# A list planner's cost table: durations from the traces, form changes, a shared port, and a smaller reserve for matmuls

## The chip, the cores and the metric

The kernel runs on one core of a Trainium2 chip. The metric is the device time of one execution in microseconds; of the kernel before, three runs gave a median of 1301.49 us (1301.43 to 1301.89). The engines are named as in the profile: PE (TensorE, matmuls), PEld (its weight loads), DVE (VectorE), ACT (ScalarE), POOL (GpSimd) and SP (SyncE, which issues the DMAs). Each engine works off its own instructions strictly in the order in which the program was written for it, and waits where an input isn't there yet.

## The reference

A residual block of a language model, on 512 tokens of width 1024. Two token mixers run side by side on the normalised input: HGRN2 (8 heads of 128, a gated linear recurrence computed in chunks of 32) and RWKV-7 (16 heads of 64, a recurrence with a rank-one correction of the state). Their outputs are projected, gated by sigmoids, summed and projected again; a residual and a gated ConvFFN follow. Cut to what matters here:

```python
z = xn @ w_in                                   # all projections of both mixers and the gates
# HGRN2: q, f, v, g -> o_a, chunkwise with decays
y_a = (rmsnorm(o_a) * silu(hg)) @ w_branch_a
# RWKV-7, one step:
sa = einsum('bhvk,bhk->bhv', state, a_t)
state = state * w_t + sa[..., None] * b_t + v_t[..., None] * k_t
y = einsum('bhvk,bhk->bhv', state, r_t)
y_b = ((groupnorm(y) + bonus) * g) @ w_branch_b
h = x + rmsnorm((sigmoid(ga) * y_a + sigmoid(gb) * y_b) @ w_out)
out = h + rmsnorm((silu(gate) * val) @ w_down)  # gate, val = causal conv of rmsnorm(h) @ w_up
```

## The kernel before

Channels lie on the 128 partitions, the 512 tokens in the free dimension. Large products are made in three matmuls with operands split into a high and a low part in a reduced fp32 type (F32R): high x high, high x low, low x high. A weight block of 128 columns arrives by DMA (`raw`), ACT casts it to `whi_t`, POOL subtracts to get `wlo_t` in two halves of 512, and 24 matmuls of 512 columns (`zps`; for the HGRN values 256 columns, `vps`) accumulate one PSUM bank. Matmuls on plain fp32 operands appear as two records each.

The program has an opening part in fixed order, a **first planned stage** (`plan.run()`, L1206), the branch projections (`yps`) in fixed order, a **second planned stage** (`plan.run()`, L1371) with the output projection (`mix`), the norms and the first blocks of the FFN, and the FFN in fixed order.

In a planned stage, the work is written as generators that run beside each other and yield one operation at a time. Those of the first stage, in order of rank (L52): `chain` (L880), `evac` (PSUM out of the projections, L1135), `solve` (L818), `front` (L702), `hgrn` (L976), `split`, `load`, `gemm` (the projections, L1155). The 16 RWKV heads go in 8 pairs, called heads here:

- `front(hb)` makes the decays, norms and scaled keys on DVE and ACT, and scores `sc` by matmuls with 64 rows; its second half waits for `chain(hb - 2)`, whose buffers `X` it reuses.
- `solve(hb)` inverts the triangular part: 14 steps of small DVE operations (`tmp`, `nb`), then four groups of small matmuls (`fps`, `dps`, `fps2`, `dps2`).
- `chain(hb)` walks 8 chunks of 64 tokens. `vp` (transposes) opens it. Each chunk has two matmuls `zy` (of `sv`), a copy to `zs` by DVE and ACT, one matmul `us` (of `zs` and `qd`), its scaling into `sv` by DVE and ACT, two matmuls `sy` (of `sv`), and their sum into the next `sv` on DVE. ACT also makes the products `sp` and copies the results to `ys` and `yb`. All the matmuls of a chunk turn through the slots of two PSUM tiles, named `us` and `yp`, 8 slots each; a matmul's record carries the tile's name. They are 128 by 128 weights by 64 columns, with the unused half of `sv` at zero. After the chunks come the group norm, `yt`, `gps`.
- `gemm` yields the projections of all heads, and at the end those of the two output gates: the first (8 blocks) is released three chunks before the end of chain 6, the second by chain 7 in the same place.

`Plan` (L78) decides the order in which the engines get these operations. `prepare` (L129) finds when an operation's inputs are ready in planned time: the end of each writer, plus `HOP` for the pair of engines (L84), plus, for a matmul whose input comes from another engine, a reserve `MARGIN` (L46). `cost` (L152) gives a planned duration. `start` (L188) is the later of ready and the engine's planned free time. `run` (L211) takes, over all generators, the operation with the least start less a bonus (L53: chain on DVE 0.3, ACT 0.2, PE 0.05 us), ties by rank; `emit` (L191) advances the engine's planned time, records the end for later readers, and issues the instruction for real, behind the last one of its engine (`seq`, L316). The planned times go nowhere else: they fix only the order of instructions on each engine.

Of the kernel before, what the change touches and what calls it, by code (L numbers as in the profile page):

```python
# [11 lines left out]
ALU = mybir.AluOpType  # L12
# [4 lines left out]
P = 128  # L17
# [25 lines left out]
NWIN = 66  # L43
NX = 2
RAWS = 1
MARGIN = 0.6  # L46
AT0 = (3, 2, 4)
XG = ((0, 0),)
MORD = ((0, 0), (1, 0), (2, 0), (3, 0), (0, 1), (1, 1), (2, 1), (3, 1))
# [8 lines left out]
class Op:  # L58
    def __init__(self, key, fn, name, args, kw):
        self.key, self.fn, self.name, self.args, self.kw = key, fn, name, args, kw  # L60
        acc = [a for n, a in kw.items() if n == "accum_out"]
        pos = [a for a in args if isinstance(a, bass.AP)]
        self.outs = pos[:1] + acc
        self.ins = pos[1:] + [a for n, a in kw.items() if isinstance(a, bass.AP) and n != "accum_out"]
        self.bounds = []
        self.ready = None
# [11 lines left out]
class Plan:  # L78
# [8 lines left out]
    def __init__(self, seq, ranks, bonus, at, gaps=False):  # L87
        self.seq, self.ranks, self.bonus, self.gaps = seq, ranks, bonus, gaps
        self.at = dict(zip("TVAGD", at))
        self.dma = 0.0  # L90
        self.wide = True
        self.hist = {}
        self.procs = []
        self.n = 0
        self.now = 0.0
# [33 lines left out]
    def prepare(self, op):  # L129
        t = 0.0  # L130
        for aps, write in ((op.outs, True), (op.ins, False)):
            for ap in aps:
                key, b = self.bound(ap)
                op.bounds.append((key, b, write))
                for c, end, eng, w in self.hist.get(key, ()):
# [4 lines left out]
                    if hit:  # L140
# [3 lines left out]
                        if op.key == "T" and eng != "T":  # L144
                            lag += MARGIN
                        elif eng == "T" and len(op.ins) > 1 and op.ins[1].free_size() == 1:
# [5 lines left out]
    def cost(self, op):  # L152
        out = op.outs[0]
        n = out.free_size()
        scalars = sum(a.free_size() == 1 for a in op.ins) if n > 1 else 0
        far = any(a.space == PSUM for a in op.ins + op.outs)
        if op.key == "T":
            n, m = op.args[2].free_size() if op.name == "matmul" else n, op.args[1].free_size()
            if op.args[1].dtype == F32R:
                op.us = n / 2400 + 0.0022  # L160
            elif op.name == "transpose":
                op.us = 0.109 if n == 128 else 0.055
            elif n == 64 and m == 64:
                op.us = 0.111 if out.offset < 64 * out.ap[0][0] else 0.0535
            elif n == 64 and m == 128:
                op.us = 0.112
            elif n == 32:
                op.us = 0.044 if m == 32 else 0.155
            else:
                op.us = 0.218  # L170
            op.wide = n > 64 or m > 64
        elif op.key == "V":
            if op.name == "tensor_reduce":
                n = op.ins[0].free_size()
            rate = 160 if op.name == "reciprocal" else 960
            if op.name in ("tensor_copy", "tensor_scalar", "tensor_single_scalar") and not far:
                rate = 1920
            op.us = 0.069 + n / rate + 0.061 * scalars
        elif op.key == "A":
            op.us = (0.051 if far else 0.093) + n / 1200 + (0.093 if scalars or len(op.outs) > 1 else 0.0)  # L180
        elif op.key == "G":
            op.us = 0.147 + n / (470 if op.name == "tensor_tensor" else 840)
            if op.kw.get("op") == ALU.pow:
                op.us = 0.3 + n * 0.165
        else:
            op.us = 0.475

    def start(self, op):  # L188
        return max(op.ready, self.at[op.key])

    def emit(self, op, start):  # L191
        end = start + op.us
        if op.key == "T":
            wide = op.wide
            if wide and not self.wide and start < self.at["T"] + 0.05:
                end += 0.053
            self.wide = wide
        self.at[op.key] = end
        if op.key == "D":
            a = op.outs[0]  # L200
            self.dma = max(end + 0.625, self.dma) + math.prod(a.shape) * 4 / 360e3
            end = self.dma + 0.9
        for key, b, write in op.bounds:
            h = self.hist.setdefault(key, [])
            if write and b is not None:
                h[:] = [e for e in h if not (b[0] <= e[0][0] and e[0][1] <= b[1] and b[2] <= e[0][2]
                                             and e[0][3] <= b[3] and b[4] in (None, e[0][4]))]
            h.append((b, end, op.key, write))
        op.ins_ = self.seq(op.key, op.fn(*op.args, **op.kw))  # L209
# [37 lines left out]
def block_kernel(ctx: ExitStack, tc: tile.TileContext, out: bass.AP, xT: bass.AP, xN: bass.AP,  # L247
# [74 lines left out]
    def mm3(o, lh, ll, rh, rl, start, stop):  # L322
        T.matmul(o, lh, rh, start=start, stop=False)  # L323
        T.matmul(o, lh, rl, start=False, stop=False)  # L324
        T.matmul(o, ll, rh, start=False, stop=stop)  # L325
# [1202 lines left out]
```

## Time and profile before

| | us |
|---|---|
| median of three runs | 1301.49 |
| the profiled execution, its own time | 1302.32 |
| its span, first to last instruction | 1300.6 |
| PE busy in the span | 1235.4 |
| DVE busy | 717.4 |
| ACT busy | 575.5 |
| POOL busy | 532.5 |
| mean granted clock of the PE | 0.959 |

The span is 1.7 us shorter than the execution's own time, which has what lies before the first and after the last instruction. Busy time of the PE counts a matmul from its start to its modelled end; since matmuls are pipelined, the next starts well before that end, and the distance of two starts says more. A clock of 0.959 is the mean over stretches at full and at half speed.

### The profile page before, as it was taken

The page shows a single profiled execution, that of the slowest core. Times are in us where ns is not written, and L with a number is a line of the kernel's source. Part 1 is how long each engine was busy: PE and PEld are TensorE (multiplying, and loading weights), DVE is VectorE, ACT ScalarE, POOL GpSimd, SP SyncE. Part 2 cuts the span into 40 slices and gives each one's busy share as a digit, 9 for nine tenths or more (in the row PEclk, how much of TensorE's full clock was granted, in tenths as well). Part 3 has the DMA queues.
Part 4 walks back from the last instruction along what each step waited for, and adds up shares of the span by engine and source line. Part 5 has one row for each costly group of instructions (what it writes and reads, how often), then busy time and mean ns, then how long its engine had stood idle before and what let it go on. Part 6 is the DMA issues. An engine that isn't in the chain of part 4 may idle for free.

```text
span 1300.6 us, 19101 instructions
## 1 busy us (share of the span) xinstructions
PE 1235.4 (95%) x7140; PEld 999.3 (77%) x7140; DVE 717.4 (55%) x1491; ACT 575.5 (44%) x1257; POOL 532.5 (41%) x444
## 2 busy tenths in 40 slices
PE   8889899999999998999798999999999999999998
PEld 6677678777778776687686788888888888888886
DVE  7988876786876968767646321334543222323213
ACT  5533464654646546354454443223544343333321
POOL 5443333252232414123042446441366675655731
PEclk9889998999999989769699999999999999999999
DMA  5122112212112112111222364337333233322432
GB/s 178 42 66 84 41 54 68 57 49 64 56 58 71 58 41 72 32 49 35 54 70 66 108 201 123 93 94 239 133 98 98 74 121 90 105 82 81 116 111 81
DMA packets 54060, 110.97 MB, mean 85 GB/s; under 512 B 21584, under 2 KB 24784, under 8 KB 53968
## 3 DMA queue, kind: packets, MB, share of 16 engines
q1 hardware_dynamic: 53968, 109.75, 27.6%
q8 instruction: 57, 0.93, 0.3%
q14 instruction: 35, 0.29, 0.1%
HBM read 100.29 MB, written 9.44 MB: 84 GB/s over the span
## 4 chain that ended last, share of the span: by engine, by line
PE 72%; DVE 15%; ACT 6%; issue 4%; POOL 2%; DMA 1%; SPq 0%; DVEq 0%; POOLq 0%; ACTq 0%
PE zps L209 17%; PE zps L323 6%; PE zps L325 6%; PE zps L324 6%; PE us L209 4%; PE dn L325 3%; PE dn L323 3%; PE dn L324 3%; PE mix L209 3%; PE sc L209 3%; PE yp L209 2%; PE vps L209 2%; PE yps L323 2%; PE yps L325 2%; PE yps L324 2%
## 5 line engine op out<-in xcount | busy, mean ns | idle before, releaser
L209 POOL TENSOR_TENSOR wlo_t<-raw,whi_t 128x512 fp32r<-128x512 f32 x134 | 184.9, 1399 | 335.2 <-ACT whi_t L209 294.2
L281 POOL TENSOR_TENSOR wlo_t<-raw,whi_t 128x1024 fp32r<-128x1024 f32 x80 | 194.4, 2437 | 96.3 <-ACT whi_t L281 95.9
L209 PE MATMUL zps<-xh,whi_t 128*128 128x512 f32 x488 | 204.9, 420 | 0.0
L209 PE MATMUL zps<-xh,wlo_t 128*128 128x512 f32 x488 | 204.0, 418 | 0.8 <-POOL wlo_t L209 0.8
L209 PE MATMUL zps<-xl,whi_t 128*128 128x512 f32 x488 | 202.7, 415 | 0.0
L281 ACT CAST whi_t<-raw 128x1024 fp32r<-128x1024 f32 x80 | 83.4, 1050 | 176.3 <-DMA raw<-wup 66.0
L1389 DVE SCALAR_TENSOR_TENSOR u<-zps,pr,u 128x511 f32<-128x511 f32 x40 | 30.0, 750 | 190.8 <-ACT u L1388 190.8
L323 PE MATMUL zps<-x2h,whi_t 128*128 128x512 f32 x320 | 125.5, 392 | 0.0
L325 PE MATMUL zps<-x2h,wlo_t 128*128 128x512 f32 x320 | 125.5, 392 | 0.0
L324 PE MATMUL zps<-x2l,whi_t 128*128 128x512 f32 x320 | 125.5, 392 | 0.0
L209 PEld LDWEIGHTS zps<-xh,wlo_t 128*128 128x128 f32 x488 | 95.2, 195 | 19.4 <-POOL wlo_t L209 1.5
L209 PEld LDWEIGHTS zps<-xl,whi_t 128*128 128x128 f32 x488 | 95.1, 195 | 18.1 <-issue 0.5
L209 PEld LDWEIGHTS zps<-xh,whi_t 128*128 128x128 f32 x488 | 95.3, 195 | 17.8
L209 ACT CAST whi_t<-raw 128x1024 fp32r<-128x1024 f32 x71 | 74.3, 1047 | 55.9 <-PE zps L209 29.2
L324 PEld LDWEIGHTS zps<-x2l,whi_t 128*128 128x128 f32 x320 | 60.2, 188 | 13.5
L325 PEld LDWEIGHTS zps<-x2h,wlo_t 128*128 128x128 f32 x320 | 60.1, 188 | 13.5
L323 PEld LDWEIGHTS zps<-x2h,whi_t 128*128 128x128 f32 x320 | 60.1, 188 | 13.4
L209 PEld LDWEIGHTS us<-sv,X 128*128 128x128 f32 x288 | 45.3, 204 | 18.7 <-ACT sv L209 7.7
L1414 POOL TENSOR_TENSOR th<-th,u 128x512 f32<-128x512 f32 x22 | 28.5, 1294 | 71.4 <-DVE u L1390 71.4
L209 PE MATMUL us<-sv,X 128*128 128x64 f32 x288 | 51.0, 289 | 5.1 <-ACT sv L209 4.1
L323 PE MATMUL yps<-oh,whi_t 128*128 128x512 f32 x128 | 50.2, 392 | 0.0
L325 PE MATMUL yps<-oh,wlo_t 128*128 128x512 f32 x128 | 50.2, 392 | 0.0
(393 smaller groups left out, 2731.2 us busy)
## 6 DMA issues: line engine op xcount, KB each, us to landing
raw<-win SPq DMA_DIRECT2D x64, 512.0 KB, 3.7
raw<-wup SPq DMA_DIRECT2D x44, 512.0 KB, 3.6
raw<-wdn SPq DMA_DIRECT2D x22, 512.0 KB, 3.5
raw<-wbr SPq DMA_DIRECT2D x16, 512.0 KB, 3.6
raw<-whi SPq DMA_DIRECT2D x8, 512.0 KB, 3.9
raw<-wout SPq DMA_DIRECT2D x8, 512.0 KB, 3.6
xt<-xT SPq DMA_DIRECT2D x8, 256.0 KB, 6.1
oa_d<-hg SPq DMA_DIRECT2D x8, 256.0 KB, 2.1
```

Of the source, the lines that this page charges most:

```text
L209: op.ins_ = self.seq(op.key, op.fn(*op.args, **op.kw))
L281: return A.copy(hi, raw), eng.tensor_tensor(lo, raw, hi.bitcast(F32), op=ALU.subtract)
L323: T.matmul(o, lh, rh, start=start, stop=False)
L324: T.matmul(o, lh, rl, start=False, stop=False)
L325: T.matmul(o, ll, rh, start=False, stop=stop)
L1389: V.scalar_tensor_tensor(u[:, 1:S], ps[:, 0 : S - 1], pc("cw1", b), u[:, 1:S], op0=ALU.mult, op1=ALU.add)
L1414: G.tensor_tensor(th, th, uv_, op=ALU.mult)
```

## The change

Nothing of the computation, and no instruction, is added or removed. `Plan` gets other numbers and two further effects, in both planned stages:

- `MARGIN`, the reserve for matmuls, goes from 0.6 to 0.45 us.
- `cost` gets other durations: F32R matmuls n/2400 + 0.0165 (0.013 up to 256 columns) in place of n/2400 + 0.0022, 1.86 times that with under 128 rows; chain matmuls 0.195 in place of 0.112; scans at 480 elements a us in place of 960; 0.07 more for a DVE operation of 64 partitions by 64 that touches PSUM; 0.11 more for an ACT operation of 256 elements on less than 128 partitions that touches PSUM.
- A matmul has a form (rows and columns of its weights, each rounded up to 32, 64 or 128). Any change of form adds 0.1 us in `emit`, and the second matmul after a return to 128 by 128 another 0.1; before, only a change from narrow (64 columns and weights of 64 at most) to wide added 0.053.
- DVE and POOL share a port in the plan: `start` moves an operation of the one that begins inside a sharing operation of the other to that one's end. Among DVE operations those share that touch no PSUM and are of the listed kinds; of POOL's all but the power.

```diff
-MARGIN = 0.6
+MARGIN = 0.45
...
-        self.wide = True
+        self.form = (P, P)
+        self.first = False
+        self.port = {"V": [], "G": []}
...
             if op.args[1].dtype == F32R:
-                op.us = n / 2400 + 0.0022
+                op.us = n / 2400 + (0.0165 if n > 256 else 0.013)
+                if op.args[1].shape[0] < P:
+                    op.us *= 1.86
...
             elif n == 64 and m == 128:
-                op.us = 0.112
+                op.us = 0.195
...
-            op.wide = n > 64 or m > 64
+            op.form = tuple(32 if x <= 32 else 64 if x <= 64 else P for x in (op.args[1].shape[0], m))
...
             op.us = 0.069 + n / rate + 0.061 * scalars
+            if op.name == "tensor_tensor_scan":
+                op.us = 0.069 + n / 480
+            if n == 64 and out.shape[0] == 64 and far:
+                op.us += 0.07
+            op.shared = not far and op.name in ("tensor_copy", "tensor_scalar", "tensor_single_scalar", "tensor_tensor",
+                                                "scalar_tensor_tensor", "tensor_tensor_scan")
         elif op.key == "A":
             op.us = (0.051 if far else 0.093) + n / 1200 + (0.093 if scalars or len(op.outs) > 1 else 0.0)
+            if far and n == 256 and out.shape[0] < P:
+                op.us += 0.11
...
     def start(self, op):
-        return max(op.ready, self.at[op.key])
+        s = max(op.ready, self.at[op.key])
+        other = {"V": "G", "G": "V"}.get(op.key)
+        if other and getattr(op, "shared", True):
+            for a, b in self.port[other]:
+                if a <= s < b:
+                    s = b
+        return s
...
         if op.key == "T":
-            wide = op.wide
-            if wide and not self.wide and start < self.at["T"] + 0.05:
-                end += 0.053
-            self.wide = wide
+            if op.form != self.form:
+                end += 0.1
+            elif self.first and op.form == (P, P):
+                end += 0.1
+            self.first = op.form == (P, P) != self.form
+            self.form = op.form
+        if op.key in self.port and getattr(op, "shared", op.kw.get("op") != ALU.pow):
+            self.port[op.key] = self.port[op.key][-3:] + [(start, end)]
```

## The prediction

> **What bounds the kernel now.** I read the page first, then the busy time in stretches cut at the milestones of the planned stage, then the chain of waits inside that stage, then the timeline of one step of the recurrent chain.
>
> ```profile
> span 1300.6 us, 19101 instructions
> PEclk9889998999999989769699999999999999999999
> ```
>
> ```profile
> core 0: us, PE busy (x) PEld busy (x) DVE busy (x) ACT busy (x) POOL busy (x), PEclk, DMA share, GB/s
> 45.00:148.00 103.00, 90.92 (x591) 73.60 (x591) 90.67 (x167) 43.26 (x75) 41.98 (x39) 0.92 0.24 70
> 148.00:302.00 154.00, 146.97 (x1074) 117.29 (x1072) 111.52 (x282) 85.26 (x231) 53.14 (x52) 0.96 0.19 56
> 302.00:448.00 146.00, 138.39 (x1006) 109.94 (x1006) 112.24 (x277) 81.55 (x229) 46.39 (x50) 0.99 0.21 61
> 448.00:544.00 96.00, 89.11 (x579) 70.27 (x579) 71.70 (x177) 45.55 (x129) 26.55 (x27) 0.91 0.14 39
> 544.00:651.00 107.00, 94.75 (x656) 76.57 (x655) 75.40 (x219) 51.55 (x157) 23.75 (x25) 0.76 0.19 52
> 651.00:723.00 72.00, 67.45 (x499) 54.04 (x498) 37.06 (x88) 38.91 (x118) 26.28 (x28) 0.98 0.20 59
> 723.00:769.00 46.00, 45.54 (x203) 36.74 (x202) 16.16 (x18) 22.69 (x32) 20.54 (x18) 1.00 0.59 185
> 879.00:952.00 73.00, 72.14 (x419) 62.60 (x418) 38.13 (x48) 35.18 (x62) 20.00 (x30) 1.00 0.51 176
> 952.00:1287.00 335.00, 335.00 (x1457) 273.39 (x1456) 94.17 (x118) 116.81 (x153) 190.94 (x106) 1.00 0.32 95
> ```
>
> The reader is to see two kernels in one. From 723 us on the PE is full at clock 1.00: 335.00 of 335 us for 1457 matmuls, 0.23 us each. Nothing the planner does can shorten that, since the diff adds and removes no instruction. The second planned stage (879 to 952) idles for 73 - 72.14 = 0.9 us. So all that can be won lies between 45 and 723 us, where no engine is full: DVE 112.24 of 146 us, ACT 81.55, and a PE whose busy figure flatters it, because a 512-wide matmul counts some 0.39 us busy while the next starts 0.23 us later. This stage is a loop of latencies. Its pace:
>
> ```profile
> L209 PE MATMUL vp<-ident,v x32: 270/273/472, 148.5 to 674.8; 128*128 128x128 f32 x32
> L209 PE MATMUL us<-zs,qd x12: 218/275/323, 374.2 to 416.9; 128*128 128x64 f32 x12
> ```
>
> `vp` opens the chain of each head: eight heads, first to last 674.8 - 148.5 = 526.3 us, over seven periods 75.2 us a head. In head 3 the eight chunks run from 374.2 to 416.9: 42.7 over seven periods, 6.1 us a chunk. A chunk has three hops through the PE (`zy`, `us`, `sy`; each logical fp32 matmul is two records). What stands in the loop is told by the chain of waits between 148 and 650:
>
> ```profile
> by line: PE zps L209 20.7%; PE us L209 8.0%; issue 7.1%; PE sc L209 5.8%; PE yp L209 5.6%; PE vps L209 3.9%; DVE ys L209 3.2%; PE hsc L209 3.1%; ACT sp L209 2.9%; DVE bk L209 2.1%; POOL wlo_t L209 2.0%; DVE sv L209 2.0%; DVE tmp L209 1.9%;
> ```
>
> `zps` and `vps` are projection matmuls, the filler between hops: 20.7% + 3.9% = 24.6% of 502 us, 123 us, in which the critical chain stands behind fillers that the plan put first. That is the pool the change can draw from.
>
> **The change, part by part.** Only emission order changes. First, what a hop looks like (head 3, 403.2 to 408.2 us; `yp` is the second bank of the same matmuls):
>
> ```profile
> 404.49 0.21 ACT L209 COPY ys<-yp 64x64 f32<-64x64 f32 x1
> 404.75 0.43 PE L209 MATMUL yp<-zs,qd 128*128 128x64 f32 x2 [0.36 <-ACT ys L209]
> 405.22 0.28 DVE L209 TENSOR_SCALAR sv<-yp,rn 64x64 f32<-64x64 f32 x1 [0.49 <-PE yp L209]
> 405.53 0.31 ACT L209 ACTIVATE sv<-yp,rn 64x64 f32<-64x64 f32 x1 [0.84 <-DVE sv L209]
> 406.50 0.55 PE L209 MATMUL yp<-sv,X 128*128 128x64 f32 x4
> 407.16 0.46 DVE L209 TENSOR_TENSOR sv<-yp,sp 64x64 f32<-64x64 f32 x2 [0.81 <-PE yp L209]
> 407.42 0.39 PE L209 MATMUL zps<-xh,whi_t 128*128 128x512 f32 x1
> 407.65 0.39 PE L209 MATMUL zps<-xl,whi_t 128*128 128x512 f32 x1
> 407.71 0.43 ACT L209 COPY yb<-yp 64x64 f32<-64x64 f32 x2 [1.87 <-DVE sv L209]
> 408.19 0.52 PEld L209 LDWEIGHTS yp<-sv,X 128*128 128x128 f32 x4 [0.35 <-ACT yb L209]
> ```
>
> Middle hop (`us` to `sy`): the last input, ACT's `sv`, ends at 405.84 and `sy` starts at 406.50, 0.66 us late, with no idle before it: it stood behind fillers. Third hop (`sy` to the next `zy`): `sv` ends at 407.62, but the matmul's weight load starts at 408.19, 0.05 us after ACT's `yb` copies end at 408.14, having idled 0.35 us. First hop (`zy` to `us`) the same: `us` starts 0.05 us after `ys` ends at 404.70. So the PE truly waits there for copies out of the same PSUM bank, a wait that neither table holds.
>
> Now the planner's own arithmetic for a middle hop, with 512-wide fillers. Before: `us` 0.112, hop to ACT 0.197, scalar operand 0.09, ACT 0.197, hop 0.27, reserve 0.6: ready at 1.466; fillers of 0.2155 are issued while they would start before 1.466 - 0.05: seven. After: 0.195 + 0.197 + 0.09 + 0.197 + 0.27 + 0.45 = 1.399, fillers of 0.2298: six. Third hop: ready at 1.246 and then 1.249, but the pair before it grows from 0.224 to 0.39, so five fillers become four; first hop likewise six become five. The new 0.2298 is what the rows show (407.42 to 407.65), the old one was short.
>
> **One filler fewer a hop is 0.23 us.** Ceiling: 64 chunks x 3 hops x 0.23 = 44 us. Middle hops: 64 x 0.23 = 14.7; some are already waiting for ACT's `sv`:
>
> ```profile
> PE us L209 <- ACT ys L209: 7.0, 13, 1.6
> PE us L209 <- ACT sv L209: 4.1, 7, 0.9
> PE yp L209 <- ACT ys L209: 2.9, 8, 0.6
> PE yp L209 <- ACT sv L209: 1.8, 3, 0.7
> ...
> PE zps L209 <- POOL wlo_t L209: 0.8, 1, 0.8
> ```
>
> These (PE's waits, 148 to 650) give 10 such of some 51 middle hops in the stretch, so I take four fifths: 12 us. Of the first hops 21 of some 51 already waited for `ys`; there, and in the third, a filler less only becomes idle PE. The rest have a little slack; 0.05 us on the 128 hops, 6 us (ends: 0, and 29 if all had it). Chain time saved: 18 us. Not all of it is the loop: a head's front part waits for the chain two heads back, its solve for the front, the next chain for the solve. I take two thirds, 12 us (ends one half and all: 9 and 18).
>
> **Front and solve.** Their PE hops (four `sc` groups, `bps`, `fps`, `dps`, `fps2`, `dps2`) are planned 0.15 us closer: some ten a head, 80 x 0.15 = 12 us, by half on the loop: 5 us with rounding to fillers down (ends 0 and 12).
>
> **The shared port.** The model follows what the trace shows:
>
> ```profile
> 400.46 0.80 DVE L209 TENSOR_TENSOR tmp<-nb 64x26 f32<-64x26 f32 x1
> 401.19 0.21 DVE L209 TENSOR_TENSOR sv<-us,sp 64x64 f32<-64x64 f32 x1
> 399.94 2.52 POOL L209 TENSOR_TENSOR wlo_t<-raw,whi_t 128x512 fp32r<-128x512 f32 x2 [3.51 <-ACT whi_t L209]
> L209 DVE TENSOR_TENSOR kj<-hk,p x32: 175/211/1326, 94.8 to 696.4; 128x64 f32<-128x64 f32 x32
> ```
>
> A DVE operation on SBUF alone took 0.80 us while POOL ran, the one that reads PSUM 0.21. `kj` has a median of 211 ns and a worst of 1326. Ordered with this in mind, a chain operation sits less often behind a blocked one; but the blocked operation still has to run. I take 2 us (ends -4 and +8). The model pushes POOL's weight splits behind DVE too; behind them stand the fillers, and the PE waited for a split once, 0.8 us, so there is room. Dearer scans, PSUM reads and 64-row matmuls in the table only move planned times; they are in these ends.
>
> **Form changes** cost PE time whichever order is taken, and the choice of the next operation doesn't look at them: 0. **Start-up** (45 to 148: DVE 90.67 of 103 us) and the second planned stage: 0, ends of 4 us either way and 1.
>
> **What it costs.** The fillers taken out of the hops must run elsewhere: at most 192 x 0.23 = 44 us of PE work. The cover is 544 to 651, where the PE got through 656 matmuls in 107 us (6.1 a us) against 1006 in 146 us (6.9 a us) at 302 to 448, and clock 0.76. It is starved there, so work deferred from earlier heads fills it. Without that cover it stands at the end, ahead of 723. I charge 4 us.
>
> The sum: -12 - 5 - 2 + 4 = -15. The profiled execution took 1302.32 us (span 1300.6 and 1.7 around it), the median of the runs is 1301.49; I set the change against the median: **1287 us** (1281 to 1297 for this case alone, since 18 + 12 us of chain and front are ends, and 4 of cost).
>
> **Rivals.** (1) **Nothing, 1299 to 1304.** If the copies, not the fillers, end most hops, every filler removed turns into an idle PE. For it: the two waits above, some 0.35 us each at 404.75 and 408.19. Against: the 0.66 us at the middle hop and the 123 us of fillers in the chain of waits. [...]
>
> (2) **Slower, 1311, up to 1325: the clock.** More and longer PE waits bring half-speed spells to stretches that are free of them. 148 to 448 (2080 matmuls) runs at 0.96 and 0.99; if it ran like 544 to 651, at 6.1 matmuls a us, it would take 341 us, 41 more than its 300. Half of that, less 11 of the gain, is +10: 1311. It decides once the clock of that stretch falls below about 0.90. For it: a PE that already idles and was halved for much of 544 to 651. Against: there the PE lacked work, while in 148 to 448 fillers are plentiful and a wait is 0.4 us. [...]
>
> (3) **Much faster, about 1265.** The fillers spread to the starved stretch and its spells go: 448 to 651 (1235 matmuls in 203 us) at 6.9 a us takes 179, 24 less; with the smaller part of the forecast, 12, that is -36.
>
> **How the numbers follow.** Forecast 0.47, nothing 0.13, slower 0.27, much faster 0.13. About 0.2% (2.6 us) is what a measurement of this kernel tells from no change. So faster 0.60, same 0.13, slower 0.27. The range 1267 to 1312 leaves out half of (3) and the upper third of (2), 0.16; the ends of the unknown terms (12 + 12 + 8 below with the rest at its value, 41 - 11 above at the worst) are what it covers or leaves out.
>
> **What would show it.** Right: `vp` first to last falls from 526 to some 512 us; `sy` starts within 0.45 us of ACT's `sv`; the share of `zps` and `vps` in the chain of waits falls; waits of the PE for `ys` and `yb` grow; everything behind the last chain keeps its length. Wrong, if the chunk stays at 6.1 us, if the clock of 148 to 448 falls, or if the gap between a head's chain and the next grows because the front, with DVE in another order, comes later.

## The result, and the profile after

The changed kernel took a median of 1296.91 us (1287.27 to 1315.42, 20 runs), the kernel before 1302.7 us (1298.91 to 1307.53, 20 runs): a ratio of 0.9948, with an interval of 0.9923 to 0.9973. So it is faster, by 0.5% or some 6 us; forecast were 15. Here and in the tables below, medians and ranges are of all runs, while ratios and their intervals leave out the few runs that the chip made in a slower state (two of the changed kernel's 20). The profiled execution took 1288.39 us, one of the quickest of its 20 runs. For that reason a second profile of the same kernel (`e1_changed_again` below, 1298.75 us) stands beside it where a size matters.

The page of the changed kernel: span, busy time, and the granted clock in 40 slices. The 21 instructions that it has more than the page before are waits on semaphores; the work is the same.

```profile
span 1286.6 us, 19122 instructions
PE 1214.3 (94%) x7140; PEld 977.4 (76%) x7140; DVE 692.1 (54%) x1491; ACT 575.4 (45%) x1257; POOL 529.9 (41%) x444
PEclk9899989999999999989999999999999999999999
```

Before, slices 15 to 20 read 8, 9, 7, 6, 9, 6, a PE at half speed for part of the time (from 552 to 574 us the mean clock is 0.50); now they read 9, 9, 9, 8, 9, 9. The same stretches as in the prediction, of the changed kernel:

```profile
core 0: us, PE busy (x) PEld busy (x) DVE busy (x) ACT busy (x) POOL busy (x), PEclk, DMA share, GB/s
45.00:148.00 103.00, 93.81 (x621) 75.10 (x621) 91.39 (x182) 46.98 (x87) 41.31 (x39) 0.93 0.23 65
148.00:302.00 154.00, 141.72 (x1054) 111.97 (x1053) 107.35 (x284) 83.91 (x233) 46.66 (x50) 0.98 0.20 58
302.00:448.00 146.00, 134.08 (x978) 106.64 (x978) 103.30 (x270) 77.34 (x219) 45.03 (x48) 0.96 0.20 58
448.00:544.00 96.00, 90.08 (x611) 68.28 (x610) 68.97 (x191) 56.85 (x163) 28.95 (x30) 1.00 0.17 50
544.00:651.00 107.00, 92.79 (x728) 75.04 (x728) 75.10 (x199) 50.68 (x137) 37.22 (x36) 0.95 0.21 62
```

Two things moved against each other. In 544 to 651 the clock rose from 0.76 to 0.95 and the PE got through 728 matmuls instead of 656, in 448 to 544 through 611 instead of 579. But in 148 to 448 it got through fewer (1054 + 978 against 1074 + 1006), and it was busy for less of that time: 275.80 us against 285.36. The clock of the two stretches was much the same (0.98 and 0.96, before 0.96 and 0.99), so the PE waited more there.

In the second profile the clock of 544 to 651 is 0.95 as well, but the PE got through only 664 matmuls. The order is the same, only shifted by some ten us: a fixed stretch then holds other work, so the 728 tell little of where the deferred fillers went.

Behind the planned stage nothing changed. The first matmul of the branch projections `yps` (the groups of that tile, with their first and last start), before and after:

```profile
L323 PE MATMUL yps<-oh,whi_t x128: 389/390/404, 790.5 to 878.0; 128*128 128x512 f32 x128
```

```profile
L345 PE MATMUL yps<-oh,whi_t x128: 389/390/404, 776.6 to 864.1; 128*128 128x512 f32 x128
```

The start of `yps` came 13.9 us earlier, and the span is 14.0 us shorter. All the PE's work in front of `yps` is the same in both kernels, so that start is a meter for the planned stage alone. Now the pace of the chain:

```profile
L231 PE MATMUL vp<-ident,v x32: 270/273/421, 137.4 to 658.3; 128*128 128x128 f32 x32
L231 PE MATMUL us<-zs,qd x12: 221/275/323, 359.6 to 398.7; 128*128 128x64 f32 x12
```

In head 3 a chunk takes (398.7 - 359.6) / 7 = 5.6 us where it took 6.1. But `vp`, first to last, fell only from 526.3 to 658.3 - 137.4 = 520.9 us, and in the second profile it is 668.3 - 138.1 = 530.2. The chunks of seven heads are shorter by 7 x 7 x 0.76 = 37 us (mean chunk 6.40 before, 5.64 after, from the `qd` matmuls of all heads). The waits from a head's last `gps` to the next head's `vp` grew by as much: added up over the seven, from 52.7 to 92.8 us. The solve is what `vp` waited for: in the mean it starts 0.3 us after the last copy of its head's solve ends. The DVE steps on `nb` took 15.8 us a head before and 21.0 after, but the steps behind them took less: from the first of them to that last copy it is 46.1 us before and 46.5 after. So the solve kept its pace, and a faster chain only waited longer for the next one.

Where does the PE wait? The waits of its weight loads from 148 to 620 us (what is waited for: us in total, times, longest). Before:

```profile
PEld us L209 <- ACT ys L209: 10.8, 17, 1.5
PEld yp L209 <- ACT ys L209: 7.9, 10, 1.9
PEld yp L209 <- ACT yb L209: 6.6, 11, 1.8
PEld us L209 <- ACT yb L209: 3.1, 8, 0.6
```

After:

```profile
PEld us L231 <- ACT ys L231: 15.1, 25, 1.1
PEld yp L231 <- ACT yb L231: 11.7, 22, 1.1
PEld yp L231 <- ACT ys L231: 11.5, 14, 1.0
PEld us L231 <- ACT yb L231: 10.5, 19, 0.9
```

Waits for ACT's copies out of the PSUM tiles `us` and `yp` went from 28.4 us (46 times) to 48.8 us (80 times). One of them, in the timeline of the changed kernel, head 3 (start, duration, engine, operation, idle before):

```profile
386.40 0.22 DVE L231 COPY zs<-yp 64x64 f32<-64x64 f32 x1 [0.20 <-PE yp L231]
386.65 0.21 ACT L231 COPY zs<-yp 64x64 f32<-64x64 f32 x1 [0.19 <-DVE zs L231]
386.87 0.70 ACT L231 ACTIVATE sp<-sv,pel 64x64 f32<-64x64 f32 x2
386.93 0.40 PE L231 MATMUL zps<-xh,whi_t 128*128 128x512 f32 x1
387.48 0.41 ACT L231 COPY ys<-yp 64x64 f32<-64x64 f32 x2
387.94 0.43 PE L231 MATMUL yp<-zs,qd 128*128 128x64 f32 x2 [0.61 <-ACT ys L231]
388.73 0.31 ACT L231 ACTIVATE sv<-yp,rn 64x64 f32<-64x64 f32 x1 [0.46 <-DVE sv L231]
389.31 0.55 PE L231 MATMUL yp<-sv,X 128*128 128x64 f32 x4
```

The matmul at 387.94 needs `zs`, which was whole at 386.86. It also writes a slot of the PSUM tile that ACT copies to `ys`, and ACT does the two `sp` first; `ys` ends at 387.89, and the matmul starts 0.05 us later. In between the PE has one filler and idles 0.61 us. At the middle hop there is no such wait: `sv` ends at 389.04, the matmul starts at 389.31.

### The profile page after: what moved, and what is told of

The parts are those of the page before. It is cut to its first block, busy times and chain, and to the rows that moved or that the text cites. A ratio compares the mean times of both kernels' runs of the same rounds, so it can differ in the third digit from the quotient of the medians.

```text
span 1286.6 us, 19122 instructions
## 1 busy us (share of the span) xinstructions
PE 1214.3 (94%) x7140; PEld 977.4 (76%) x7140; DVE 692.1 (54%) x1491; ACT 575.4 (45%) x1257; POOL 529.9 (41%) x444
## 3 DMA queue, kind: packets, MB, share of 16 engines
q1 hardware_dynamic: 53968, 109.75, 27.8%
## 5 line engine op out<-in xcount | busy, mean ns | idle before, releaser
L231 POOL TENSOR_TENSOR wlo_t<-raw,whi_t 128x512 fp32r<-128x512 f32 x134 | 181.0, 1370 | 372.4 <-ACT whi_t L231 333.7
L231 PE MATMUL zps<-xh,whi_t 128*128 128x512 f32 x488 | 202.1, 414 | 0.0
L231 PEld LDWEIGHTS us<-sv,X 128*128 128x128 f32 x288 | 42.2, 194 | 20.9 <-ACT yb L231 13.3
L231 PE MATMUL us<-sv,X 128*128 128x64 f32 x288 | 47.1, 278 | 6.4 <-ACT yb L231 3.3
```

## The experiments

Two accounts are set side by side below, worked out from the matmul records from 45 us to the first `yps`: by how much the start-to-start distances exceed those of the same shapes at full speed without a wait, once for matmuls that start at full clock (**waits**, form changes among them) and once for those at half (**half speed**). In the profile of before, the 512-column matmuls of a projection start 0.23 us apart at full clock (229.37 and 229.60) and 0.43 us apart at half (529.57 and 530.00).

| profile | first `yps`, us | waits, us | half speed, us |
|---|---|---|---|
| before | 790.5 | 121.6 | 59.2 |
| changed, first profile | 776.6 | 144.6 | 22.9 |
| changed, second (`e1_changed_again`) | 786.8 | 140.5 | 36.2 |
| changed, reserve 0.6 (`e3_margin_060`) | 766.0 | 122.2 | 33.7 |
| changed, wait planned (`g1_bank_045`) | 742.2 | 111.4 | 21.5 |
| before, wait planned (`h1_before_bank`) | 747.1 | 104.4 | 33.6 |

Each group of runs below was measured beside runs of its own of the kernel before; their medians were 1301.68, 1302.06, 1304.28 and 1303.31 us in the four groups, and the ratios go by them.

The theory after the result: the reserve was also the cover for a wait that the plan does not know, so that cutting it turned fillers into idle PE and gave back most of what the rest brought. The rivals: the solve, whose `nb` steps grew, sets the end now; or another part of the change, such as the port model, does the harm.

**First group: parts of the change undone.** The changed kernel once more, unaltered:

> The changed kernel, unaltered, for a second profile and its spread beside the variants. Theory CLOCK (the runs of the changed kernel differ because spells of half PE clock fall differently each time): times spread over 1287 to 1310, each run's time follows its mean granted clock at some 11 us per 0.01, and the second profile shows the same chunk (5.6 us) whatever its clock. Theory LOOP (the chain got faster, 6.4 to 5.6 us a chunk, but the solve's DVE steps and the front got slower and handed it back): heads 74 to 75 us apart again. If the spread came from something other than the clock, time and clock would not go together.

Without the port model:

```diff
-        if other and getattr(op, "shared", True):
+        if False:
```

> The changed kernel with start() left as before, so DVE and POOL are planned without the shared port; all else new. Theory PORT (the port model moves the solve's small SBUF operations back behind POOL's splits, and that is why its 14 steps grew from 15.8 to 21.0 us a head): the steps come back to about 16 us, the heads move to some 71 us apart, and the time falls by 10 to 20 us. Theory LOOP with DVE crowding (a faster chain takes DVE's turns, whatever the port): the steps stay at 20 to 21 us, the time within 5 us, and DVE operations that meet POOL are longer, as before the change.

With the old reserve:

```diff
-MARGIN = 0.45
+MARGIN = 0.6
```

> The changed kernel with the old reserve of 0.6; table, form changes and port new. Theory LOOP (the chain is no longer what the loop waits for): the chunk goes back toward 6.0 us, but the heads stay 74 to 76 us apart and the time within 4 us of the changed kernel. Theory CHAIN (the prediction's: two thirds of the chain's time reach the end): 0.4 us a chunk, 25 us of chain in all, some 15 us slower. If the waits of the PE bring on the half clock, a larger reserve gives a higher clock and less spread between runs.

With DVE priority for the solve:

```diff
-BONUS = {("chain", "V"): 0.3, ("chain", "T"): 0.05, ("chain", "A"): 0.2}
+BONUS = {("chain", "V"): 0.3, ("chain", "T"): 0.05, ("chain", "A"): 0.2, ("solve", "V"): 0.3}
```

> The changed kernel with a bonus of 0.3 us for the solve's DVE operations, the same as the chain's. Theory LOOP: the solve's 14 steps shorten from 21 to 16 us or less, the next chain starts earlier, the heads come to some 72 us apart and the time falls by 10 to 15 us. Theory FRONT (the front, which then loses DVE's turns, is as much on the loop): the steps shorten but the front's second half grows by as much, and the time stays within 4 us.

| run | median us (range, runs) | ratio to before (interval) |
|---|---|---|
| changed, unaltered | 1296.1 (1289.42 to 1312.82, 12) | 0.9943 (0.9918 to 0.9968) |
| no port model | 1316.1 (1310.1 to 1323.39, 6) | 1.0137 (1.0098 to 1.0175) |
| reserve 0.6 | 1278.73 (1272.92 to 1285.12, 6) | 0.9836 (0.9798 to 0.9873) |
| solve bonus | 1304.52 (1300.28 to 1308.19, 12) | 1.0024 (1.0003 to 1.0045) |

The first row repeats the result, and its profile shows the cost again. The stretch of the chains before, in the changed kernel's second profile, and with the old reserve:

```profile
148.00:620.00 472.00, 445.22 (x3168) 355.51 (x3166) 350.33 (x869) 250.11 (x696) 147.33 (x152) 0.93 0.18 53
```

```profile
148.00:620.00 472.00, 432.23 (x3131) 342.17 (x3130) 329.25 (x867) 248.72 (x699) 138.93 (x148) 0.95 0.19 54
```

```profile
148.00:620.00 472.00, 444.20 (x3201) 354.87 (x3201) 342.87 (x905) 255.25 (x721) 150.37 (x151) 0.95 0.19 56
```

The first number after the 472.00 is PE busy: idle are 26.8 us before, 39.8 changed, 27.8 with the reserve back at 0.6. So **the smaller reserve costs the change 1296.1 - 1278.7 = 17 us**; without it the change is worth 1.6%, some 21 us. Neither expectation had this: one said within 4 us, the other 15 us slower. Taking the port model away costs 20 us, which tells against the port as the culprit. The steps on `nb` took some 16 us a head again, as was expected, but the waits from `gps` to `vp` still added up to 94 us and the time rose: the longer `nb` steps are not what held the heads back.

The solve bonus answers the rival on the chain. It did what it should: `nb` took 11 us a head, and the last chunk of the last head, the last start in this row, came at 687.4 instead of 701.7 us (711.6 in the changed kernel's second profile).

```profile
L231 PE MATMUL us<-zs,qd x96: 217/275/421, 139.3 to 687.4; 128*128 128x64 f32 x96
```

And the kernel was slower, 1304.52. The chain ended 14 to 24 us earlier, yet the first `yps` came at 788.9, later than in both profiles of the changed kernel: from the last chunk to `yps` it took 101.5 us instead of 75. (Another 7.5 us were lost behind the first `yps`; why is not known.) **When the chain ends is not what sets the time.**

**Second group: parts of the change put into the kernel before, and another reserve.** The reserve alone in the kernel before:

```diff
-MARGIN = 0.6
+MARGIN = 0.45
```

> The kernel before with the reserve at 0.45 and nothing else of the change. Theory RESERVE (the smaller reserve takes fillers out of hops that end at ACT's copies, so they become idle PE, and the work left over stands behind the last chain): the PE's waits between 150 and 620 us grow by 15 to 20 us and the time is 10 to 17 us above the kernel before. Theory TABLE (a smaller reserve only hurts beside the dearer table): chunk 0.2 us shorter, time within 4 us of before or below it.

The port model alone in the kernel before (`port` in `start` and `emit`, `op.shared` in `cost`, as in the change):

> The kernel before with the shared port modelled and nothing else. Theory PORT-GAIN (the port model is what the change gains by: leaving it out of the changed kernel cost 19 us): 12 to 20 us below the kernel before, DVE busy some 15 us lower. Theory TOGETHER (the port model only helps a plan whose PE is priced right): within 5 us of before.

The changed kernel with a reserve larger than that of before:

```diff
-MARGIN = 0.45
+MARGIN = 0.75
```

> The changed kernel with a reserve of 0.75. Theory RESERVE: waits of the PE fall a little further, the chunk grows by 0.1 to 0.3 us, and the time is within 5 us of that with 0.6 (1279), at any rate well below the changed kernel (1296). Theory BEST-AT-060 (fillers in front of a chain that is late again cost what the waits save): 1288 to 1300.

The durations and the form changes at the old reserve, without the port model:

```diff
-MARGIN = 0.45
+MARGIN = 0.6
...
-        if other and getattr(op, "shared", True):
+        if False:
```

> The changed kernel with the old reserve of 0.6 and without the port: durations and form changes alone. Theory PORT-GAIN: the time is back near the kernel before, 1295 to 1305. Theory TABLE-GAIN (true durations alone keep fillers and chain in step): 1280 to 1290.

| run | median us (range, runs) | ratio to before (interval) |
|---|---|---|
| before, reserve 0.45 | 1300.58 (1293.51 to 1307.08, 12) | 0.9999 (0.9968 to 1.0031) |
| before, port model | 1302.11 (1297.04 to 1303.91, 12) | 1.0007 (0.9983 to 1.0031) |
| changed, reserve 0.75 | 1284.93 (1283.14 to 1286.67, 6) | 0.9884 (0.9845 to 0.9922) |
| durations and forms, 0.6 | 1297.57 (1292.98 to 1320.36, 12) | 0.9974 (0.9946 to 1.0002) |

The reserve alone and the port alone are each worth nothing that can be measured, the durations with the form changes 0.3% at most likely. Only durations, forms and port together at the old reserve give 1.6%. The parts do not add up one by one. By the theory the reserve alone should have cost time in the kernel before too, and it did not. Its one profile has the cost all the same, hidden by a gain: PE idle in 148 to 620 went up to 472 - 436.07 = 35.9 us, while half speed fell (28 us from 154 us on to `yps`, against 52 before).

```profile
148.00:620.00 472.00, 436.07 (x3174) 347.47 (x3172) 342.75 (x876) 251.04 (x702) 152.24 (x152) 0.96 0.19 54
```

The port model alone says once more that the chain's end is not the meter. The `us` matmuls of all heads, in the kernel before and with the port model: the last chunk starts 20 us later, and the time is the same.

```profile
L209 PE MATMUL us<-zs,qd x96: 217/275/476, 154.2 to 723.0; 128*128 128x64 f32 x96
L220 PE MATMUL us<-zs,qd x96: 217/275/476, 153.0 to 743.0; 128*128 128x64 f32 x96
```

The reserve of 0.75 came out between the two expectations, 6 us above 0.6, and the intervals of the two overlap. So a still larger reserve for all matmuls brings nothing more, though in 148 to 620 us the waits for the copies still add up to 34.3 us (36.8 with 0.6).

**Third group: the wait itself.** If the unplanned wait for the copies is what the reserve covered, then telling the plan of it must pay, and make the reserve matter little. One line in `prepare`: a matmul that writes a slot of `us` or `yp` is held, in planned time, until the readers of any slot of that tile are done. (The plan counts `vp`, `yt` and `gps`, which take turns in the same PSUM space, to `us`, so they are held too.)

```diff
-                        hit = (w or write) and self.meet(b, c)
+                        hit = (w or write) and self.meet(b, c) or (write and not w and op.key == "T" and key in ("us", "yp"))
```

> The changed kernel (reserve 0.45), with one thing more in the plan: a matmul that writes the chain's two PSUM tiles is planned behind every earlier read of that tile, whatever the columns, as the trace shows it to wait for ACT's ys and yb copies. Theory RESERVE (the smaller reserve loses because the first and third hop truly end at these copies, which the plan doesn't know, so fillers were taken out of a wait): the waits of the PE at these hops (44 of 64 and 50 of 56) fall by half or more, the PE's excess between 147 and 620 us falls from 110 to some 92 us, and the time to 1275 to 1285. Theory NOISE-OF-ORDER (any other order gives another time, the copies are not the reason): 1290 to 1305.

The same at a reserve of 0.6:

> The same with the reserve at 0.6. Theory RESERVE: hardly a wait left at the first and third hop, chunk 6.0 to 6.3 us, time 1270 to 1285. Theory NOISE-OF-ORDER: anywhere from 1275 to 1305, without the waits telling it.

The wait made shorter instead of planned: in `chain`, ACT's `ys` copies go ahead of its `sp` products, at a reserve of 0.6, with nothing told to the plan.

```diff
+            for h in range(2):
+                yield A1.copy(ys[hs[1 - h], n], zy[h][hs[1 - h]])
...
-            for h in range(2):
-                yield A1.copy(ys[hs[1 - h], n], zy[h][hs[1 - h]])
```

> The changed kernel with the reserve at 0.6 and, in the chain, ACT's ys copies ahead of its sp products instead of behind them. Theory RESERVE/COPIES (the first hop ends at ys, and two products of 0.35 us stand before it on ACT): the first hop falls by up to 0.7 us, from 2.32 to some 1.7, the waits there go, chunk some 5.3 us, and the time is 5 to 15 us below that with 0.6 alone (1279). If idle PE and not the chain's length counts, it gains by the waits alone: 64 x 0.39 = up to 25 us less excess, part of it taken back by earlier heads being short of fillers.

The changed table and port at 0.6 with the old rule for forms:

```diff
-            if op.form != self.form:
-                end += 0.1
-            elif self.first and op.form == (P, P):
-                end += 0.1
+            wide = max(n_.free_size() for n_ in op.args[1:3]) > 64
+            if wide and not self.wide and start < self.at["T"] + 0.05:
+                end += 0.053
+            self.wide = wide
```

> The changed kernel with the reserve at 0.6 and the old rule for form changes; durations and port new. If the form changes (some 290, 0.1 to 0.3 us each) matter to the plan: up to the time of the kernel before, 1290 to 1302. If the durations and the port together are what helps: within 5 us of 1279.

| run | median us (range, runs) | ratio to before (interval) |
|---|---|---|
| wait planned, 0.45 | 1253.31 (1250.01 to 1253.9, 4) | 0.9605 (0.9579 to 0.9631) |
| wait planned, 0.6 | 1252.43 (1245.94 to 1254.93, 6) | 0.9588 (0.9557 to 0.9619) |
| copies first, 0.6 | 1257.58 (1254.18 to 1260.39, 5) | 0.964 (0.9614 to 0.9667) |
| old form rule, 0.6 | 1290.22 (1285.71 to 1295.15, 6) | 0.9893 (0.9866 to 0.9919) |

With the wait in the plan the kernel is 4% faster than before, eight times what the change brought, and 0.45 or 0.6 no longer makes a difference. The waits of the weight loads in 148 to 620 us, with the wait planned at 0.45:

```profile
PEld us L231 <- ACT ys L231: 8.6, 13, 2.1
PEld yp L231 <- ACT yb L231: 5.1, 15, 0.9
PEld us L231 <- ACT yb L231: 4.8, 12, 0.8
PEld yp L231 <- ACT ys L231: 4.0, 11, 2.1
```

48.8 us have become 22.5. And the PE is busy for 452.92 of the 472 us, idle 19.1:

```profile
148.00:620.00 472.00, 452.92 (x3331) 363.34 (x3331) 348.83 (x941) 265.13 (x743) 157.84 (x162) 0.97 0.20 59
```

It gets through 3331 matmuls there instead of 3158. The two times lie some 20 us below the ranges that were expected (1275 to 1285 and 1270 to 1285). Putting the copies first gives nearly the same without telling the plan anything: the first hop fell from 2.32 us in the mean to 1.97 (1.7 was expected), and the hops there that waited over 0.15 us fell from 44 to 10. Two ways to remove one wait, one size of gain, which no reserve between 0.45 and 0.75 reached. So it is the wait for the copies that cost the time, and not the order that one edit happens to bring. The form rule is worth about 0.6% at 0.6 (0.9893 against 0.9836), but the two intervals touch.

**Fourth group: the wait alone.** The one line in the kernel before, with its old table, no port and 0.6:

> The kernel before (old table, reserve 0.6, no port, old form rule) with the chain's PSUM tiles planned as in the two runs with the bank: a matmul that writes them stands behind every earlier read. Theory WAIT-ALONE (the unplanned wait is the whole of it, the table hardly matters): 1250 to 1265, as with the changed kernel. Theory WAIT-AND-TABLE (knowing the wait only helps when the fillers in front of it are priced right): 1280 to 1300, and the waits at the first and third hop stay at a third of the hops or more.

Both cures on the changed kernel, at 0.45:

> The changed kernel (reserve 0.45) with both: the wait in the plan, and ACT's ys copies ahead of its sp products. Theory IDLE-PE (only idle and half-speed PE counts, and either edit removes the idle at the first hop): 1245 to 1258, no better than one of them by more than 8 us, chunk some 5.4 us. Theory CHAIN (a shorter chain is worth two thirds of itself): 0.6 us a chunk less than with the wait alone, 38 us of chain, so 20 to 25 us, about 1230.

| run | median us (range, runs) | ratio to before (interval) |
|---|---|---|
| before, wait planned | 1261.13 (1258.24 to 1265.28, 5) | 0.9685 (0.9656 to 0.9714) |
| changed, wait planned, copies first | 1250.1 (1245.85 to 1259.38, 6) | 0.9606 (0.9569 to 0.9642) |

One line in the old plan gives 3.2%; the whole change gave 0.5%. With the line in place the change still adds something: 0.9605 against 0.9685. The last run beats both kernels, but not clearly the two at 1252 to 1253. The kernel before with the line also settles what the meter is. Its head 3, chunks first to last:

```profile
L209 PE MATMUL us<-zs,qd x12: 217/274/323, 372.7 to 421.1; 128*128 128x64 f32 x12
```

(421.1 - 372.7) / 7 = 6.9 us a chunk, and 6.7 in the mean of all heads: **the chunk is slower than before (6.1 and 6.4), and the kernel is 42 us faster.** The chain as a whole is not slower, though. The waits from `gps` to the next `vp` added up to 25 us instead of 52.7, and the last chunk starts at 704.4 instead of 723.0:

```profile
L209 PE MATMUL us<-zs,qd x96: 217/275/474, 154.0 to 704.4; 128*128 128x64 f32 x96
```

That is 19 us, less than half of the gain, and the changed kernel, whose chain ended at about the same time (701.7 and 711.6), starts its `yps` 30 to 40 us later. The meter is how much of the PE's work is done by then: more fillers go into the hops, and 3419 matmuls into 148 to 620 instead of 3168:

```profile
148.00:620.00 472.00, 455.54 (x3419) 370.91 (x3419) 367.48 (x948) 262.13 (x734) 153.54 (x161) 0.97 0.20 58
```

The last run says the same: with both cures a chunk takes 5.7 us in the mean against 6.0 with the wait planned alone, and the last chunk starts at 670.2 instead of 681.8, but the time is only 3 us less, as theory IDLE-PE had it.

The table of the two accounts adds a limit. In the changed kernel the line took off 29 to 33 us of waits and 1 to 15 us of half speed. In the kernel before it took off 17.2 us of waits and 25.6 us of half speed: there more than half of the gain came by way of the clock, and why less half speed goes with fewer waits is not shown.

## Why the prediction was right and wrong

**The sign was right, the size was not:** 6 us of the 15, at the very edge of the forecast case's own 1281 to 1297, and made up of other terms than its sum. The sign was in part luck: what the prediction summed up came out as 19 to 23 us more waits, and the gain came from half speed, which its sum does not hold.

- "Nothing the planner does can shorten that", of the time from 723 on: right. The start of `yps` and the end moved by the same 14 us.
- "**One filler fewer a hop is 0.23 us**": more came than was forecast. A middle hop went from a mean of 1.87 us to 1.70, close to the 0.18 that four fifths of a filler make. The other two were given 0.05 each, and went from 2.55 to 2.20 and from 1.99 to 1.75. Per chunk that is 0.76 us and over 64 chunks 49, where the step had 18.
- "**I take two thirds, 12 us**": here the prediction failed. It priced chain time as kernel time. Of what the chunks saved, hardly anything shortened the loop: `vp` first to last is 520.9 and 530.2 us where it was 526.3, not 512, because the solve kept its pace and the waits between the heads grew by 40 us. More to the point, three runs show that the chain's end is not the meter: with the solve bonus it comes 14 to 24 us earlier and the kernel is slower; with the port model alone it comes 20 us later and the time is the same; with both cures it comes 12 us earlier than with one, for 3 us. In this kernel the work of the PE ahead of `yps` is fixed and the projections fill whatever is left; the time is that work plus what the PE waits and what it loses at half speed.
- "**I charge 4 us**" for the fillers taken out of the hops: the second failure, of the same root. That the deferred fillers went to 544 to 651, as said, is not shown: it took 728 matmuls in one profile and 664 in the other, for 656 before. And the hops that lost them idled: between `sy` and `zy` the PE waited over 0.15 us in 47 of 56 hops, against 20 before. In 148 to 620 the idle PE grew by 13 to 14 us (26.8 to 39.8 and 41.2), and putting the reserve back alone was worth 17.
- "A wait that neither table holds": seen, and left as a remark. The prediction said that in the first and third hop a filler less "only becomes idle PE" and then counted none of it. The trace after the change has that wait too (the matmul 0.05 us after `ys`, at 387.94). That the plan's lack of it costs some 40 us only the runs showed: one line that adds it took 43 us off the changed kernel and 42 off the kernel before.
- **Front and solve**, 5 us: not gained. The solve's `nb` steps got longer, 15.8 to 21.0 us a head, its later steps shorter, and the whole stayed at 46 us; the run with the solve bonus shows that shortening the `nb` steps does not pay.
- **The shared port**, 2 us from -4 to +8: alone nothing (1.0007), but with the new durations 18 to 20 us, at either reserve. The step took parts to be worth the same alone and together. Why the two need each other was not found out. Of DVE beside POOL the trace of before shows this: of the 112 `tmp` made from `nb`, the 57 that met no POOL operation took at most 0.21 us, and of the 55 that did the slowest took 1.72; the sums `sv` of `us` or `yp` and `sp`, which read PSUM, took at most 0.23 us with POOL or without.
- **Form changes**, 0: about 7 us (0.6%) at a reserve of 0.6, hardly told from nothing. That they take PE time is in the matmul records of before, which have 292 of them from 45 us to the first `yps`: at full clock a chain matmul of 64 columns is followed 0.112 us later by another of its form and 0.205 us later by a `sc` matmul of 64 rows (medians of 372 and 19 pairs).
- **Rival 1, nothing**: its mechanism came, waits for the copies up from 28.4 to 48.8 us; by the run with the old reserve it took back 17 of some 21 us: most of the gain, not all.
- **Rival 2, the clock falls**: it did not. 148 to 448 stands at 0.98 and 0.96, in the second profile at 0.95 and 0.97, all far from 0.90. That waits of the PE bring half speed, as it supposed, no run shows: the waits grew by 23.0 and 18.9 us while half speed fell.
- **Rival 3, the spells go**: its mechanism came, and it is what the measured gain is made of. By the account above, half speed fell by 36.3 us in the first profile and 23.0 in the second, waits grew by 23.0 and 18.9: the sums, -13.3 and -4.1, are the 13.9 and 3.7 by which `yps` came earlier. The prediction had it as a case apart and not as a term beside the waits.
- Of the signs named, the waits for `ys` and `yb` grew as said, and what lies behind the first `yps` kept its length, while the stretch from the last chunk to `yps` grew from 67.5 to 75 us; `vp` did not fall to 512; `sy` starts 0.47 us after `sv` in the mean and 0.53 in the second profile (0.55 before), so it missed the 0.45; of the signs of being wrong, the gap between a head's chain and the next did grow, from 52.7 to 92.8 us over seven; the share of `zps` in the chain of waits can't be read, since that chain of the changed kernel does not reach back into this stage.

What stays open: why half speed fell. No run set the PE's load and nothing else, so "the deferred fillers fed the starved stretch" is an argument, not shown. And each edit reorders the whole stage, so gains of under some 5 us between two orders say little of a cause; 17, 20 and 42 us do.

## What to carry to other kernels

Where one engine has a fixed amount of work ahead of a fixed tail and fillers to hand, count what it loses (waits and half speed) up to that tail, not the length of the latency chain. Before trimming a planner's reserve, look for what it silently covers: here a wait for another slot of the same PSUM tile, which belonged in the plan as a dependency, and after that the reserve hardly mattered. Corrections of a cost table are worth trying together: the port alone gave nothing and the durations with the forms 0.3%, together they gave 1.6%.

## What the runs showed of the hardware

One program, in one order, ran anywhere between 1287 and 1306 us on one core (18 of its 20 runs), and its time followed the granted clock: the changed kernel's span was 1285.6 us at a mean clock of 0.984, 1294.6 at 0.974 and 1303.6 at 0.965. Half-speed spells therefore differ from run to run, and a gain of half a per cent needs the clock beside it. At the same mean clock of 0.967 the changed kernel's spans were 1303.2 and 1304.4, those of the kernel before 1291.2, 1291.3, 1292.1, 1292.4 and 1293.4: by this reading the change made the order some 12 us worse, and the kernel came out ahead by a better clock. With the wait planned in the changed kernel the gain is not one of the clock: the run at 0.6 had a span of 1252.6 at 0.972, the changed kernel's second profile 1296.9 at the same 0.972, here in the view of the cores (span and mean granted clock):

```profile
core 0: 1296.9 us, clock 0.972
```

In the profile of before, the PE ran at half speed for 52 of the 107 us from 544 to 651 (a mean clock of 0.76), and no two matmuls that follow each other started more than 2.1 us apart there. What sets the granted clock is not shown.
